# The low parts of the dense weights: subtracted by VectorE alone instead of by VectorE and GpSimd

## The chip, the cores and the metric

The kernel runs on one core of a Trainium2 chip. The metric is the time of one execution on the device in microseconds (us), the median over three runs. Differences are given as a ratio to the kernel before.

## The reference

One block of a streaming encoder, batch 1, 512 tokens of 1024 features, all in float32:

```python
h = rms_norm(x, attn_norm_g);  u = h @ w_in                    # 1024 -> 2048
u_pool, u_q, u_k, u_v = split(u)                               # 512 columns each
y_pool = (trailing means of u_pool over 2/4/8/16 tokens - u_pool) @ w_pool * pool_scale
o = softmax(q1 k1) v - lam * softmax(q2 k2) v                  # 4 heads, two maps each, partial rotary
x += concat(y_pool, rms_norm(o)) @ w_out
x += cross_attention(rms_norm(x), rms_norm(mem), w_cq, w_ckv, w_co)   # 256 rows of memory
x += moe(rms_norm(x))                                          # the top 4 of 32 experts, clamped SwiGLU
return rms_norm(x, final_norm_g)
```

## The kernel before

The program has two stretches. The **dense part** (norms, pooling, differential attention, cross attention, router; about the first 400 us) computes its products in two parts: every operand is split into a high part in float32r (`hi`, rounded by ScalarE) and a low part (`lo`, what is left), and a product is three matmuls, hi*hi, hi*lo and lo*hi (`mm3`). The **experts** follow, one after the other, with plain float32 matmuls; nothing in that stretch is changed.

The dense weights come in 28 pieces of 512 rows by 512 columns (1 MB): 8 of `w_in`, 8 of `w_ckv`, 4 each of `w_out`, `w_cq` and `w_co`. `w_load` (L159) has SyncE issue the DMA of a raw piece into a buffer; `w_split` turns it into `w_hi` and `w_lo`, in two halves `b` = 0 and 1 of 128 partitions x 1024 elements: ScalarE copies to `w_hi` (L117), and an elementwise subtraction of two operands in SBUF gives `w_lo` (L118). `w_next` hands a piece that is ready to the matmuls, splits one ahead and loads one more. The raw piece's buffer is free when both subtractions are done. The normed memory's values, `cv`, are split once in the same way, in two halves `cvs` (L508).

In the kernel before, half 0 is subtracted by VectorE and half 1 by GpSimd, but for the very first piece, which VectorE does alone. So of the 56 subtractions of weights VectorE has 29 and GpSimd 27; both of `cvs` are GpSimd's. Beside these, GpSimd has in the dense part only constants at the start, one small memset (L426) and one small product for the router (L812).

Each engine executes its instructions in the order of the built program, and that order comes from a scheduler: in the dense part it places every instruction by its own estimate of when its inputs and its engine are ready, apart from a short pinned piece at the start. So a change of engine for some instructions also moves others. In the experts the order of TensorE is that of the code.

Names that the rows use: `u` is the pooling branch's product `pps` times the rows' norm (L433), `win` and `mixed` its trailing sums (L572 to L578), `yp` the product with `w_pool`, `y_l` a low part of the block's mixed output (L121). `lams` are the four lambda vectors (L543 to L552). `rot` and `turned` are the rotary step of queries and keys (L280 by ScalarE, L281 to L286 by VectorE), whose result TensorE transposes (`qkT`, L111); `qTl` and `kTl` are low parts of the transposed queries and keys. In the differential attention, `s` are scores, L624 and L625 mask them and take their maximum `mx`, L627 scales it, ScalarE takes the exponential (L629), L631 to L634 make the probabilities `pr`, TensorE transposes them to `aT`, ScalarE copies these to `a` (L643), and L192 to L200 and L658 to L661 (`orstd`, `oss`, `on`) norm the head's output. The products of the memory (`ckps`, `cvps`) are filled in between the steps of this attention.

Of the kernel before, what the change touches and what calls it, by code (L numbers as in the profile page):

```python
# [39 lines left out]
def two_pi_parts():  # L40
    """2*pi cut into parts of at most 12 significant bits."""
    rest, parts = 2 * math.pi, []
    for bits in (9, 20, 31):
        q = math.floor(rest * 2 ** bits) / 2 ** bits
        parts.append(q)
        rest -= q
    parts.append(float(np.float32(rest)))
    return parts


class Halves:
    """A [1024, n] operand, rows k * 128 + p, as float32r high and low parts in four tiles."""
# [8 lines left out]
class Block:  # L61
# [8 lines left out]

    def later(self, n, fn):
        """fn's instructions come n steps of matmuls later."""
        self.todo.append([n, fn])
# [14 lines left out]
    def queued(self):  # L88
        """TensorE's instructions of this block are issued in the order of the program."""
# [9 lines left out]
    @contextmanager  # L99
    def when(self, flag):  # L100
        """TensorE's instructions of this block run if the flag, in a register of its, is set."""
        with self.queued(), self.tc.If(flag):  # L102
            yield
# [9 lines left out]
    def split(self, hi, lo, src, scale=None, lo_engine=None):  # L113
        """src (times a scale per partition) = hi + lo, exactly, both float32r."""
        nc = self.nc
        if scale is None:
            self.pin(nc.scalar.activation(hi, src, AF.Copy))  # L117
            self.pin((lo_engine or nc.vector).tensor_tensor(lo, src, hi.bitcast(F32), op=OP.subtract))  # L118
# [12 lines left out]
    def warm(self, n):  # L131
        """n products that nobody reads: TensorE keeps its clock through a wait."""
        t = self.bank("warm")
        for _ in range(n):
            self.mm(t[:, :P], self.ones, self.ones, start=True, stop=True)
# [13 lines left out]
    # weights of the dense part, in halves [512 rows, 512 columns], in the order of their use  # L149
# [12 lines left out]
    def w_split(self, first=False):  # L162
        if not self.w_raw:
            self.w_load()
        if self.w_raw:
            t = self.w_raw.pop(0)
            hi, lo = self.slot("w_hi", [P, 4, 512], F32R), self.slot("w_lo", [P, 4, 512], F32R)
            for b in range(2):
                c = slice(2 * b, 2 * b + 2)
                self.split(hi[:, c], lo[:, c], t[:, c], lo_engine=self.nc.gpsimd if b and not first else None)  # L170
# [11 lines left out]
    def pin(self, ins):  # L182
        """Where order matters: ins is not issued before what its engine got so far."""
# [3 lines left out]
    def rstd(self, ss, n, name, out=None):  # L187
        """(sum of squares / n + eps) ** -0.5: a first guess from the bits, three Newton steps."""
# [14 lines left out]
    def turn(self, x, g, dst, i, a):  # L203
        """Half a of the features of x [128 rows, 512], times the gain g, to the halves dst, columns
        i * 128 + row."""
# [9 lines left out]
    def squares(self, x, ss):  # L215
        """ss = the sums of the squares of the rows of x."""
# [3 lines left out]
    def gain(self, v, name):  # L220
        """A gain as columns, row k * 128 + p in [p, k]."""
# [16 lines left out]
    def rotary_tables(self, r):  # L238
        """cos, sin [128, 4, 8] of the angles of the positions, and those times r."""
# [32 lines left out]
    def rotary(self, dst, src, i, r=None):  # L272
        """dst [128, 512] = src (PSUM), times r if it is given, with its heads' first 16 columns
        turned."""
# [17 lines left out]
    def tokens_by_piece(self, act, evac, name, before=None, ahead=1):  # L292
        """act.T @ piece for the next two halves of the weights: evac(i, bank) per 128 tokens."""
# [14 lines left out]
    def features_by_piece(self, act, evac, name):  # L308
        """(act.T @ piece).T for the next two halves: evac(f, bank) per 128 features."""
# [11 lines left out]
    def memory_keys(self, act, evac):  # L321
        """The same for the 256 rows of the memory, in steps."""
# [30 lines left out]
    def dense(self):  # L353
# [23 lines left out]
        # the first norm: its gain goes into h, its rows' scales to what comes of h  # L377
# [24 lines left out]
        self.w_split(True)  # L402
# [35 lines left out]
        # queries and keys: turned, then features on partitions  # L438
# [19 lines left out]
        # differential attention, with the memory's keys and values among it  # L458
# [19 lines left out]
        # x += y @ w_out  # L478
# [28 lines left out]
        for n in range(2):  # L507
            self.split(cvs[0][:, n], cvs[1][:, n], cv[:, n], lo_engine=nc.gpsimd)  # L508
# [16 lines left out]
    def columns(self):  # L525
        """pool_scale and subln_g as columns."""
# [11 lines left out]
    def lambdas(self):  # L538
        """The weight of the second map."""
# [14 lines left out]
    def pooling(self, u, cols, y):  # L554
        """Trailing means of u [channel, group, token] less u, times w_pool, to y."""
# [6 lines left out]
        # 1 / (t + 1) for the first tokens  # L562
# [39 lines left out]
    def diff_attention(self, qT, kT, v, y, scale, fill):  # L602
# [3 lines left out]
        def scores(qb, h):  # L606
            n = (qb + 1) * P
            q = slice(qb * P, n)
            # the two maps, [128, n] each, in a bank each
# [73 lines left out]
    def cross_attention(self, cq, ckT, cv, scale):  # L683
# [30 lines left out]
        def turn(i, pr):  # L714
            # pT: tile of two heads, (head, half of the memory)
# [36 lines left out]

    def moe_constants(self):
        nc, c, jp = self.nc, self.cst, self.jp
        # strictly earlier tokens, all tokens
# [10 lines left out]
        # what the one-hot slots pick of a token: its number in two parts, its gate in three, one  # L766
# [14 lines left out]
        # powers of two, for a word of flags per 16 experts  # L781
# [3 lines left out]
        # the gate-up biases, rows (hi or lo, half, expert), and what picks a row of them  # L785
# [33 lines left out]
    def logits(self, i, c):  # L819
        """The sums of squares and the logits of 128 tokens, as far as half c of x goes. The norm  # L820
        is left to route, its gain to what reads the rows and to the router's weights."""
# [19 lines left out]
    def route(self):  # L841
        """The four experts of all tokens, and their places."""
# [37 lines left out]
    def gates(self):  # L880
        """The softmax over the four, in three parts of eight bits."""
# [17 lines left out]
    def count(self):  # L899
        """The experts' numbers of tokens; a word of flags per 16 experts: which have more than  # L900
        64; the number of further passes over an expert with more than 96."""
# [12 lines left out]
        # (pass, expert): a pass over slots 96 pass + 97 and on that has tokens  # L914
# [11 lines left out]
    def load_down_biases(self):  # L926
        """In the room of what the first expert's gate and up get later."""
# [7 lines left out]
    def round_down_biases(self, raw):  # L935
        """The biases of down, a half of the columns each, in rows (high, low, high)."""
# [7 lines left out]
    def down_biases(self, bd):  # L944
        """These and the gates, in rows (high, high, low)."""
# [10 lines left out]
    def one_hots(self, pt, slot_no, tv):  # L956
        """pt [128, 2, 6] = what the slots pick of the tokens"""
# [8 lines left out]
    def slots(self, pt, n):  # L966
        """For the slots of n experts: rows to gather, gates, rows of y to add to."""
# [11 lines left out]
        # a slot without a token matches none  # L979
# [16 lines left out]
    def normed(self, xg):  # L996
        """The rows gathered, times what their norm divides by."""
# [16 lines left out]
    def first_features(self):  # L1014
        """The same for expert 0, straight from x: the others' rows are gathered meanwhile. And the
        gates."""
# [18 lines left out]
    def load_gate_up(self, e, n=KT):  # L1035
        """Rows 8 p + j in tile j, for j < n."""
# [9 lines left out]
    def load_down(self, e):  # L1046
        """Rows 256 j + 2 p + b in tile j."""
# [7 lines left out]
    def swiglu(self, gate, up, n):  # L1055
        """(up + 1) * gate * sigmoid(1.702 gate), clamped; columns (j p b) go to (j b p)."""
# [11 lines left out]
    def biases(self, pick):  # L1068
        """Gate-up accumulators that hold the biases: slots 0..63 on partitions (half of the
        columns, slot), slots 64..95 on (quarter of the columns, slot)."""  # L1070
# [37 lines left out]
    def sums(self):  # L1108
        """Room for what a pair of experts adds: y of slots 0..63 and the tokens' one-hot rows per
        expert, both for slots 64..95 of the two."""  # L1110
# [5 lines left out]
    def down(self, aT, aT2, dn, gat, tok, cond, a, c, last=False):  # L1116
        """gate * act @ w_down and the tokens' one-hot rows: to a for slots 0..63, in partitions
        (high or low part, slot), to c for slots 64..95."""
# [37 lines left out]
    def combine(self, i, parts):  # L1156
        """x += what the parts (rows of y, their tokens' one-hot rows) add to 128 tokens"""
# [243 lines left out]
```

## Time and profile before

| what | value |
|---|---|
| time, median of 3 runs | 1555.97 us (1555.66 to 1556.44) |
| span of the profiled execution, first to last instruction | 1551.3 us |
| TensorE busy | 1491.1 us, 96% of the span |
| VectorE busy | 694.4 us, 45% |
| ScalarE busy | 385.2 us, 25% |
| GpSimd busy | 115.5 us, 7% |
| mean granted clock of TensorE | 0.986 of full speed |

The time of a run is taken around the whole launch, the span from the trace of one execution; they differ by 4.7 us here. A busy share is a mean over very different stretches, so the rows further down are taken by stretch.

### The profile page before, as it was taken

The page shows a single profiled execution, that of the slowest core. Times are in us where ns is not written, and L with a number is a line of the kernel's source. Part 1 is how long each engine was busy: PE and PEld are TensorE (multiplying, and loading weights), DVE is VectorE, ACT ScalarE, POOL GpSimd, SP SyncE. Part 2 cuts the span into 40 slices and gives each one's busy share as a digit, 9 for nine tenths or more (in the row PEclk, how much of TensorE's full clock was granted, in tenths as well). Part 3 has the DMA queues.
Part 4 walks back from the last instruction along what each step waited for, and adds up shares of the span by engine and source line. Part 5 has one row for each costly group of instructions (what it writes and reads, how often), then busy time and mean ns, then how long its engine had stood idle before and what let it go on. Part 6 is the DMA issues. An engine that isn't in the chain of part 4 may idle for free. (4 is left out here: it accounts for less than half of the span.)

```text
span 1551.3 us, 22087 instructions
## 1 busy us (share of the span) xinstructions
PE 1491.1 (96%) x8852; PEld 752.4 (49%) x8852; DVE 694.4 (45%) x1650; ACT 385.2 (25%) x691; POOL 115.5 (7%) x81
## 2 busy tenths in 40 slices
PE   9998999999999999999999999999999999999994
PEld 7777778888733434343433434333343433333332
DVE  6847775352453434243453434343343434444234
ACT  5344544353011111111222111121112111121213
POOL 2212112301000000000000000000000000000001
PEclk9999999999899999999999999999999999999997
DMA  6132124155788998989999998989989999999911
GB/s 218 62 112 82 55 86 150 55 221 203 258 331 319 386 386 341 376 338 399 372 401 404 407 402 326 408 344 360 399 341 390 374 401 373 392 373 389 409 42 56
DMA packets 84152, 455.36 MB, mean 294 GB/s; under 512 B 14169, under 2 KB 14690, under 8 KB 34882
## 3 DMA queue, kind: packets, MB, share of 16 engines
q1 hardware_dynamic: 79170, 438.90, 72.0%
q0 software_dynamic: 3472, 12.29, 2.5%
q10 hardware_dynamic: 1392, 2.51, 0.4%
q8 instruction: 86, 1.41, 0.4%
q14 instruction: 32, 0.26, 0.0%
HBM read 449.45 MB, written 4.21 MB: 292 GB/s over the span
## 5 line engine op out<-in xcount | busy, mean ns | idle before, releaser
L107 PE MATMUL gu<-gu,xT 128*64 128x512 f32 (+1 forms) x3200 | 603.6, 599 | 1.2 <-PEq L102 1.2
L107 PEld LDWEIGHTS gu<-gu,xT 128*64 128x64 f32 (+1 forms) x3200 | 167.9, 127 | 344.9 <-issue 338.4
L107 PE MATMUL down<-dnw,aT 128*32 128x256 f32 (+1 forms) x2288 | 305.0, 478 | 3.3 <-PEq L102 2.5
L107 PEld LDWEIGHTS down<-dnw,aT 128*32 128x32 f32 (+1 forms) x2288 | 108.6, 122 | 175.4 <-issue 149.8
L1105 ACT ACTIVATE aT<-actT 128x512 f32<-128x512 f32 x64 | 27.9, 487 | 542.2 <-PE actT L111 542.2
L1171 DVE TENSOR_TENSOR x<-comb,x 128x1024 f32<-128x1024 f32 x68 | 82.9, 1220 | 131.7 <-PE comb L107 131.7
L1059 DVE TENSOR_SCALAR g<-gu 128x256 f32<-128x256 f32 (+1 forms) x64 | 33.3, 553 | 229.1 <-PE gu L107 193.6
L121 DVE SCALAR_TENSOR_TENSOR yb<-down,gat,yb 32x256 fp32r<-32x256 f32 x128 | 61.6, 481 | 129.5 <-ACT yb L120 129.4
L120 ACT ACTIVATE yb<-down,gat 32x256 fp32r<-32x256 f32 x128 | 59.7, 466 | 224.3 <-PE down L107 118.3
L992 POOL DMA_INDIRECT xg<-x_rows,gi x31 | 28.5, 919 | 1004.9 <-DVE gu L1062 600.0
L107 PE MATMUL comb<-ya,yb 128*128 128x512 f32 x256 | 97.0, 420 | 3.7 <-PEq L102 2.8
L118 POOL TENSOR_TENSOR w_lo<-w,w_hi 128x1024 fp32r<-128x1024 f32 x27 | 71.4, 2647 | 264.1 <-ACT w_hi L117 210.0
L107 PEld LDWEIGHTS comb<-ya,yb 128*128 128x128 f32 x256 | 47.9, 187 | 63.3 <-DVE x L1171 37.8
L121 DVE SCALAR_TENSOR_TENSOR ya<-down,gat,ya 64x512 fp32r<-64x512 f32 x64 | 48.0, 750 | 26.3 <-ACT ya L120 26.2
L117 ACT ACTIVATE w_hi<-w 128x1024 fp32r<-128x1024 f32 x56 | 57.0, 1053 | 10.9 <-DMA w<-in_w_ckv_dram 3.5
L970 DVE COPY slots<-slots 128x12 f32<-128x12 f32 x32 | 5.5, 171 | 118.4 <-PE slots L107 118.4
L1061 ACT ACTIVATE s<-g 128x256 f32<-128x256 f32 (+1 forms) x64 | 32.4, 521 | 87.6 <-DVE g L1059 85.8
L120 ACT ACTIVATE ya<-down,gat 64x512 fp32r<-64x512 f32 x64 | 43.8, 685 | 32.3 <-DVE ya L121 23.8
L107 PE MATMUL comb<-yb,ohc 128*128 128x512 f32 x128 | 50.2, 392 | 0.0
L118 DVE TENSOR_TENSOR w_lo<-w,w_hi 128x1024 fp32r<-128x1024 f32 x29 | 42.1, 1453 | 15.8 <-ACT w_hi L117 13.4
L1065 DVE TENSOR_TENSOR g<-gu,s 128x512 f32<-128x512 f32 (+1 forms) x64 | 48.7, 840 | 0.0
L111 PEld LDWEIGHTS xgT<-ident,xg 96*128 96x128 f32 x248 | 29.9, 202 | 30.6 <-ACT xg L999 16.3
(340 smaller groups left out, 1827.2 us busy)
## 6 DMA issues: line engine op xcount, KB each, us to landing
gu<-in_w_gu_dram SPq DMA_DIRECT2D x256, 1024.0 KB, 12.6
dnw<-in_w_down_dram SPq DMA_DIRECT2D x128, 1024.0 KB, 9.6
w<-in_w_ckv_dram SPq DMA_DIRECT2D x8, 1024.0 KB, 5.1
w<-in_w_in_dram SPq DMA_DIRECT2D x7, 1024.0 KB, 8.1
w<-in_w_out_dram SPq DMA_DIRECT2D x4, 1024.0 KB, 5.0
w<-in_w_cq_dram SPq DMA_DIRECT2D x4, 1024.0 KB, 7.2
w<-in_w_co_dram SPq DMA_DIRECT2D x4, 1024.0 KB, 5.1
x<-in_x_dram SPq DMA_DIRECT2D x8, 256.0 KB, 6.2
```

The lines of the kernel that those rows point to most:

```text
L107: self.pin(self.nc.tensor.matmul(*a, **k))
L111: self.pin(self.nc.tensor.transpose(*a))
L117: self.pin(nc.scalar.activation(hi, src, AF.Copy))
L118: self.pin((lo_engine or nc.vector).tensor_tensor(lo, src, hi.bitcast(F32), op=OP.subtract))
L120: nc.scalar.activation(hi, src, AF.Copy, scale=scale)
L121: nc.vector.scalar_tensor_tensor(lo, src, scale, hi.bitcast(F32), op0=OP.mult, op1=OP.subtract)
L992: nc.gpsimd.indirect_dma_start(out=xg, out_offset=None, in_=self.rows, in_offset=bass.IndirectOffsetOnAxis(ap=gi, axis=0))
L1059: nc.vector.tensor_scalar(g, gate, LIMIT, None, op0=OP.min)
L1061: nc.scalar.activation(s, g, AF.Sigmoid, scale=ALPHA)
L1065: nc.vector.tensor_tensor(g.rearrange("s (j b p) -> s j p b", p=P, b=2), r(up), r(s), op=OP.mult)
L1105: nc.scalar.activation(aT, pt[:, :n], AF.Copy)
L1171: self.nc.vector.tensor_tensor(xi, ps, xi, op=OP.add)
```

## The change

The function that splits loses its choice of engine; VectorE now subtracts both halves of every piece and both halves of the memory's values. (Comments are deleted too, which changes no instruction.)

```diff
-    def split(self, hi, lo, src, scale=None, lo_engine=None):
-        """src (times a scale per partition) = hi + lo, exactly, both float32r."""
+    def split(self, hi, lo, src, scale=None):
+
         nc = self.nc
         if scale is None:
             self.pin(nc.scalar.activation(hi, src, AF.Copy))
-            self.pin((lo_engine or nc.vector).tensor_tensor(lo, src, hi.bitcast(F32), op=OP.subtract))
+            self.pin(nc.vector.tensor_tensor(lo, src, hi.bitcast(F32), op=OP.subtract))
...
-    def w_split(self, first=False):
+    def w_split(self):
...
             for b in range(2):
                 c = slice(2 * b, 2 * b + 2)
-                self.split(hi[:, c], lo[:, c], t[:, c], lo_engine=self.nc.gpsimd if b and not first else None)
+                self.split(hi[:, c], lo[:, c], t[:, c])
...
-        self.w_split(True)
+        self.w_split()
...
         for n in range(2):
-            self.split(cvs[0][:, n], cvs[1][:, n], cv[:, n], lo_engine=nc.gpsimd)
+            self.split(cvs[0][:, n], cvs[1][:, n], cv[:, n])
```

In the built program VectorE has 29 instructions more (27 `w_lo`, 2 `cvsl`) and GpSimd 29 fewer. Three places of VectorE's order show how they come to stand.

The first is VectorE in the pooling branch, from the `u` of the first group on. Before:

```order
L433 TENSOR_TENSOR u<-pps,r_bcast 128x512
L572 TENSOR_TENSOR win<-u 128x511
L573 COPY win<-u 128x1
L118 TENSOR_TENSOR w_lo<-w,w_hi 128x1024
L576 TENSOR_TENSOR mixed<-win,ti 128x1
L578 SCALAR_TENSOR_TENSOR mixed<-win,u 128x511
L433 TENSOR_TENSOR u<-pps,r_bcast 128x512
```

The same place of the changed kernel:

```order
L433 TENSOR_TENSOR u<-pps,r_bcast 128x512
L572 TENSOR_TENSOR win<-u 128x511
L573 COPY win<-u 128x1
L118 TENSOR_TENSOR w_lo<-w,w_hi 128x1024
L433 TENSOR_TENSOR u<-pps,r_bcast 128x512
L576 TENSOR_TENSOR mixed<-win,ti 128x1
L578 SCALAR_TENSOR_TENSOR mixed<-win,u 128x511
L577 TENSOR_TENSOR mixed<-mixed,u 128x1
L572 TENSOR_TENSOR win<-u 128x511
L573 COPY win<-u 128x1
L118 TENSOR_TENSOR w_lo<-w,w_hi 128x1024
L433 TENSOR_TENSOR u<-pps,r_bcast 128x512
```

The second `u` has moved ahead of two rows of `mixed`, and the piece's second `w_lo` stands ahead of the third `u`.

The second place is VectorE where the queries' rotary step begins, after the pooling branch's last `mx`. Before:

```order
L118 TENSOR_TENSOR mx<-mixed,mx 128x512
L546 TENSOR_TENSOR lams<-lams 128x2x64
L121 SCALAR_TENSOR_TENSOR y_l<-yp,cols,y_h 128x512
L269 TENSOR_TENSOR cos_sin<-cos_sin,scales 128x64
L548 TENSOR_REDUCE lame<-lams 128x2
L551 TENSOR_TENSOR lam<-lame 128x1
L552 TENSOR_SCALAR lam<-lam 128x1
L281 TENSOR_TENSOR rot<-qps,cos_sin 128x64
```

In the changed kernel:

```order
L118 TENSOR_TENSOR mx<-mixed,mx 128x512
L269 TENSOR_TENSOR cos_sin<-cos_sin,scales 128x64
L281 TENSOR_TENSOR rot<-qps,cos_sin 128x64
L282 TENSOR_TENSOR rot<-qps,cos_sin 128x64
L283 TENSOR_TENSOR rot<-qps,cos_sin 128x64
L284 TENSOR_TENSOR rot<-qps,cos_sin 128x64
L546 TENSOR_TENSOR lams<-lams 128x2x64
L285 TENSOR_TENSOR turned<-rot 128x8x8
L548 TENSOR_REDUCE lame<-lams 128x2
L286 TENSOR_TENSOR turned<-rot 128x8x8
```

The four rows of `rot` no longer stand behind `lams`, but the first row of `turned` does; the `y_l` that stood here has moved up, and so have two `w_lo` of one piece, where one stood. On SyncE's queue the DMA of the last piece of `w_in` now stands ahead of the DMAs of `lams`, behind which it stood before; it waits there for products of `pps`.

The third place is VectorE at the start of the attention, where the keys' last rotary step meets the first scores. Before, from the last row of `turned` to `kTl` (ahead of these rows the order is that which the changed kernel shows below):

```order
L286 TENSOR_TENSOR turned<-rot 128x8x8
L118 TENSOR_TENSOR w_lo<-w,w_hi 128x1024
L631 RECIPROCAL sums<-sums 128x2
L632 TENSOR_TENSOR sums<-sums,lam 128x1
L118 TENSOR_TENSOR kTl<-qkT,kTh 128x4x128
```

In the changed kernel, from the maximum of the first scores on:

```order
L625 TENSOR_REDUCE mx<-s 128x1 x2
L118 TENSOR_TENSOR w_lo<-w,w_hi 128x1024
L627 TENSOR_SCALAR mx<-mx,scales 128x2
L281 TENSOR_TENSOR rot<-kps,cos_sin 128x64
L282 TENSOR_TENSOR rot<-kps,cos_sin 128x64
L283 TENSOR_TENSOR rot<-kps,cos_sin 128x64
L284 TENSOR_TENSOR rot<-kps,cos_sin 128x64
L285 TENSOR_TENSOR turned<-rot 128x8x8
L286 TENSOR_TENSOR turned<-rot 128x8x8
L118 TENSOR_TENSOR w_lo<-w,w_hi 128x1024
L631 RECIPROCAL sums<-sums 128x2
L118 TENSOR_TENSOR w_lo<-w,w_hi 128x1024
```

Up to `turned` the order is that of before; the added `w_lo` stand behind it, ahead of `kTl`.

## Rows read from the trace of the kernel before

**Rows 1.** The page's first part: busy time, share of the span, instructions.

```profile
PE 1491.1 (96%) x8852; PEld 752.4 (49%) x8852; DVE 694.4 (45%) x1650; ACT 385.2 (25%) x691; POOL 115.5 (7%) x81
```

**Rows 2.** Windows by stretch: busy us per engine, TensorE's granted clock, DMA share, GB/s.

```profile
122.00:210.00 88.00, 74.58 (x466) 62.07 (x466) 69.39 (x184) 44.77 (x104) 19.07 (x7) 0.92 0.24 80
210.00:400.00 190.00, 186.63 (x1064) 159.32 (x1065) 84.73 (x164) 72.44 (x138) 36.22 (x18) 1.00 0.44 160
400.00:1551.00 1151.00, 1117.27 (x6765) 439.61 (x6764) 458.87 (x1068) 210.12 (x366) 35.48 (x34) 0.99 0.88 349
60.00:80.00 20.00, 18.31 (x80) 14.82 (x81) 19.86 (x65) 4.71 (x7) 2.58 (x1) 1.00 0.02 4
```

**Rows 3.** Timeline of TensorE: start, duration, in brackets the idle time before and its releaser.

```profile
61.69 0.50 PE L107 MATMUL pps<-hh,w_hi 128*128 128x512 f32 x1 [2.36 <-DVE u L433]
...
86.06 0.63 PE L111 MATMUL qkT<-ident,turned 128*128 128x128 f32 x4 [2.70 <-DVE turned L286]
...
125.65 0.90 PE L111 MATMUL qkT<-ident,turned 128*128 128x128 f32 x4 [3.66 <-DVE turned L286]
...
141.70 0.39 PE L107 MATMUL s<-kTh,qTh 64*128 64x256 f32 x2 [2.24 <-ACT pr L629]
...
177.19 0.69 PE L107 MATMUL s<-kTh,qTh 64*128 64x384 f32 x1 [3.16 <-ACT a L643]
...
199.91 0.30 PE L111 MATMUL aT<-ident,pr 128*128 128x128 f32 x1 [1.75 <-DVE orstdt L198]
```

**Rows 4.** TensorE's waits, 0 to 400 us: total us, times, longest.

```profile
PE qkT L111 <- DVE turned L286: 6.8, 3, 3.7
...
PE aT L111 <- DVE pr L634: 1.9, 3, 0.9
```

**Rows 5.** Timeline of GpSimd at one of its subtractions.

```profile
56.89 2.40 POOL L118 TENSOR_TENSOR w_lo<-w,w_hi 128x1024 fp32r<-128x1024 f32 x1 [6.17 <-ACT w_hi L117]
```

**Rows 6.** Timeline of VectorE: operations beside those of GpSimd, `u` and `lams`.

```profile
56.94 3.43 DVE L118 TENSOR_TENSOR w_lo<-w,w_hi 128x1024 fp32r<-128x1024 f32 x1
...
60.96 0.68 DVE L433 TENSOR_TENSOR u<-pps,r_bcast 128x512 f32<-128x512 f32 x1
...
74.81 2.37 DVE L573 COPY win<-win 128x8 f32<-128x8 f32 x1
...
83.10 0.29 DVE L546 TENSOR_TENSOR lams<-lams 128x128 f32<-128x128 f32 x1 [1.56 <-DMA lams<-in_lambda_k_dram]
...
119.88 2.62 DVE L118 TENSOR_TENSOR w_lo<-w,w_hi 128x1024 fp32r<-128x1024 f32 x1
...
122.42 2.30 DVE L627 TENSOR_SCALAR mx<-mx,scales 128x2 f32<-128x2 f32 x1
...
138.68 1.88 DVE L627 TENSOR_SCALAR mx<-mx,scales 128x2 f32<-128x2 f32 x1
...
163.58 2.16 DVE L632 TENSOR_TENSOR sums<-sums,lam 128x1 f32<-128x1 f32 x1
...
173.00 2.09 DVE L193 TENSOR_SCALAR orstdt<-orstdv 128x4 int32<-128x4 int32 x1
```

**Rows 7.** VectorE's `w_lo`: duration min/median/max in ns, first and last start.

```profile
L118 DVE TENSOR_TENSOR w_lo<-w,w_hi x29: 1212/1225/3427, 8.4 to 363.6; 128x1024 fp32r<-128x1024 f32 x29
```

**Rows 8.** The page's costliest groups, the weights' subtractions: busy, mean ns | idle before.

```profile
L118 POOL TENSOR_TENSOR w_lo<-w,w_hi 128x1024 fp32r<-128x1024 f32 x27 | 71.4, 2647 | 264.1 <-ACT w_hi L117 210.0
...
L118 DVE TENSOR_TENSOR w_lo<-w,w_hi 128x1024 fp32r<-128x1024 f32 x29 | 42.1, 1453 | 15.8 <-ACT w_hi L117 13.4
```

**Rows 9.** Windows right behind three of TensorE's gaps, columns as above.

```profile
125.80:129.30 3.50, 3.50 (x20) 3.05 (x19) 2.89 (x9) 0.60 (x1) 0.00 (x0) 0.51 0.41 87
142.90:146.30 3.40, 3.40 (x17) 2.98 (x18) 3.37 (x4) 1.41 (x3) 1.70 (x1) 0.50 0.31 119
177.00:183.90 6.90, 6.71 (x18) 5.31 (x19) 4.73 (x20) 2.15 (x6) 0.00 (x0) 0.51 0.00 0
```

**Rows 10.** The page's DMA issues: KB each, median us from issue to landing.

```profile
w<-in_w_in_dram SPq DMA_DIRECT2D x7, 1024.0 KB, 8.1
```

## The prediction

> **What bounds the kernel now.** I read the busy shares first. TensorE works 96% of the span, every other engine less than half, and GpSimd 7% [rows 1]. So a change pays only where TensorE stands still or runs at half clock, and I took the windows by stretch next [rows 2]. In the experts, 400 to 1551 us, TensorE is busy 1117.27 of 1151 us at a granted clock of 0.99; in 210 to 400 it is busy 186.63 of 190. Between 122 and 210 us, the attention, it is busy 74.58 of 88 us at a clock of 0.92, while VectorE works 69.39. In 60 to 80 us VectorE works 19.86 of 20. The experts hold nothing that the change touches, and TensorE bounds them: what the dense part gains or loses moves their start, one to one.
>
> Then the waits of TensorE in the dense part. Its largest gaps stand in its timeline with what ended them [rows 3]: 2.36 us at 61.69 (`u`), 2.70 at 86.06 and 3.66 at 125.65 (`turned`), 2.24 at 141.70 (the exponential `pr`), 3.16 at 177.19 (`a`), 1.75 at 199.91, 15.9 us together. The waits add 0.45 more for `turned` (6.8 less the two) and three for `pr` with 1.9 in sum [rows 4]. All end with VectorE, or with ScalarE behind it. None names a `w_lo`: the subtractions are early enough, and matter only by whom they hold up.
>
> The last view is VectorE beside GpSimd [rows 5, 6]. Half a piece takes VectorE 1.22 us (median) [rows 7]; GpSimd takes 2.65 [rows 8]. But operations of VectorE that start beside one of GpSimd's end only after it. The `w_lo` at 56.94 takes 3.43 us: GpSimd's runs from 56.89 to 59.29, and VectorE ends 1.08 us behind it. The copy of eight columns at 74.81 takes 2.37 us, the scaling of two numbers per partition at 122.42 2.30, and 138.68, 163.58 and 173.00 show 1.88, 2.16 and 2.09 for operations that else take some 0.2. I count 18 such stretched operations in the dense part, by my estimate about 28 us together; seven of them are in these rows (119.88 with 2.62 is the seventh), the others repeat the pattern.
>
> **What the change does, part by part.** It removes 29 subtractions from GpSimd, for which TensorE does not wait, and with them the stretches, some 28 us of VectorE's time. It adds 29 x 1.2 = 35 us to VectorE. That is +7 us on an engine that idles most of the time; what counts is the place of each. ScalarE's copies stay as they are. A piece is done about as early as before (two in sequence, 2.4 us, against one of GpSimd's, 2.65), so raw buffers come free no later, and the loads stay where they are or move up. The two `cvsl` and the 13 `w_lo` behind 210 us lie beside a TensorE that is 98% busy there [rows 2] and waits for none of them; I cost them at nothing. Without that cover they would cost 15 x 1.2 = 18 us.
>
> Place by place, as the order shows them:
> - 61.69, 2.36 us. The stretch of the `w_lo` (3.43 - 1.22 = 2.2 us) goes, and the second `u` stands right behind the first `w_lo`: it ends at 56.94 + 1.22 + 0.68 = 58.8 instead of 60.96 + 0.68 = 61.6 [rows 6]. That is 2.8 earlier, so the gap goes whole: **2.4**.
> - 86.06, 2.70 us. VectorE is full ahead of it. Two stretches go (2.2 each, 56.94 and 74.81), two more `w_lo` stand in the way (2.4), and a `y_l` has moved up (0.7): 1.3 us sooner. Also `rot` no longer stands behind `lams`, whose wait of 1.56 us at 83.10 falls out of its way. That makes up to 3 us, but TensorE itself comes 2.4 sooner. The gap shrinks by 0.5 to 1.8; I take **1.0**.
> - The 0.45 for `turned` behind it comes after another stretched row: **0.45**.
> - 125.65, 3.66 us. Ahead of `turned` stand the `w_lo` at 119.88 with 2.62 us and the scaling at 122.42 with 2.30. Without GpSimd they take 1.2 and 0.2, and the added `w_lo` stand behind `turned`: 1.4 + 2.1 = 3.5, less a little, **3.4**. Behind these `w_lo` waits `kTl`, 1.2 us per `w_lo` later; scores of the last keys need it, and TensorE has products of the memory ahead of them.
> - 141.70, 2.24 us. The scaling at 138.68 loses 1.65 of its 1.88 us, but the second `w_lo` stands ahead of it: 1.65 - 1.2 = **0.45**.
> - The three waits for `pr`, 1.9 us in sum. Each comes after a stretch as that at 163.58 (2.16 - 0.16 = 2.0), and each has one `w_lo` more ahead: up to 0.8 each, or what there is; **1.5**.
> - 177.19, 3.16 us. The stretch of 1.9 at 173.00 goes, and the scaling that lets the exponential start, with `a` behind it in ScalarE's order, now stands ahead of both `w_lo`; some of it is taken by a row of probabilities that has moved ahead: **1.6**.
> - 199.91, 1.75 us: a `w_lo` stretched as the one at 56.94 (2.1) less one of 1.2, and 0.3 by the order of the rows: **1.2**.
>
> That is 12.0 us. Each can be lost again at the next wait: from below I bound the sum by a third, 4 us, since VectorE is full at 60 to 80 us and 79% busy at 122 to 210; from above by all of the gaps named, 18.2 us.
>
> **The clock.** Three gaps are followed by stretches at half clock, 1.2 instead of 2.4 GHz: 0.51 for 3.5 us behind 125.65, 0.50 for 3.4 behind 141.70, 0.51 for 6.9 from 177.0 on [rows 9]. Half of each is lost: 1.7, 1.7 and 3.4 us. The gaps of 2.36 and 2.70 us have no such stretch behind them (60 to 80 us: 1.00 [rows 2]), and one of 2.24 has, so a gap's length alone does not decide. I take back the first (its gap falls to about 0.3 us), 1.7 us, and nothing for the others; from above, all 6.8.
>
> **A rule that speaks against the change.** In 60 to 80 us VectorE is 99% busy [rows 2]. The Trainium skill (Perfetto Trace Analysis, Optimizing Scalar/DVE Operations) says that with VectorE saturated, giving work to GpSimd may make sense, though the port that the two share can undo that. By its first half the two `w_lo` taken back here would cost 2.4 us at 86.06 instead of the 1.0 that I credit, and the sum would be 8.6. The rows show the second half: the two stretches cost VectorE 4.4 us, more than the two `w_lo`.
>
> **The sum.** The profiled execution spans 1551.3 us, with 4.7 us around it by the median. 12.0 + 1.7 = 13.7 us; of these I keep an estimated 12, since many rows change places and some of it is lost again: 1551.3 - 12 = 1539.3 in the span and 1544.0 in time. Less than 0.2% (3.1 us) I call no change, about what a measurement of this kernel can tell.
>
> **The rivals.**
> - No change, within 0.2%. The work added eats the stalls removed, +35 against -28 us on VectorE. Where TensorE waits for a chain of scaling, exponential and `pr`, a `w_lo` of 1.2 in the chain is little better than a stretch; only 61.69 and 125.65 gain (5.8), and half of it is waited for elsewhere: about 1553. For it: the net at 141.70 is only 0.45. Against it: at 125.65 no added `w_lo` stands ahead. Chance 0.13.
> - Part of the gain: 61.69, 86.06 and 125.65 give 6.8, the attention behind gives nothing: 1549, to 1552.9 with a little lost. Chance 0.15.
> - More gain: the half-clock stretches behind 141.70 and 177.19 go as well, 1.7 + 3.4 = 5.1: about 1539, or down to 1533 if all gaps close. For it: these gaps shrink to 1.8 and 1.6. Against it: 2.24 was enough for one. Chance 0.14.
> - Slower. `turned` at 86.06 stands behind `lams`, whose DMAs now queue behind the last 1 MB of `w_in`, and such a piece takes 8.1 us to land [rows 10]. If it starts only when `lams` could, `lams` lands up to 8 us later than at 83.1, `turned` 5 us later than now, and a half-clock stretch follows: the 2.4 of 61.69 and the 1.0 here are lost, 5 + 1.7 to 3.4 come on top, 3.4 at 125.65 come off, and the rest gives nothing: 1559 to 1561. It decides once `lams` lands over 5 us later. For it: VectorE has no slack there. Against it: the piece waits for products of `pps`, which end soon after the gap at 61.69, long before `lams`. Chance 0.08.
>
> **How the numbers follow.** The main case, 1540 to 1549, has 0.50. Under 1536 I put 0.07, over 1556 0.14; the range is 1536 to 1556. Faster by over 0.2%: 0.50 + 0.15 + 0.14 = 0.79; within: 0.13; slower: 0.08.
>
> **What the next profile would show.** If right: no stretched operation on VectorE; `w_lo` x56 there at 1.2 us each; TensorE's gaps at 61 and 125 us gone or under 0.5, that for the first `turned` near 1.7; the stretch 122 to 210 us shorter by some 6 to 8 with a clock over 0.92; the experts' length as before. Wrong if `w_lo` takes VectorE over 1.25 us beside other work, if gaps of over 2 us stand at new places of the attention, or if the experts wait for their weights.

## The result, and the profile after

The changed kernel takes 1530.47 us (median of 4 runs, 1529.61 to 1531.18) against 1555.82 for the kernel before beside it (4 runs, 1554.26 to 1556.44): a ratio of 0.9844, with an interval of 0.9833 to 0.9856. It gained 25.4 us where 12 were predicted; the time lies below the range. The direction was right and so was the mechanism, the size was not. In 40 more runs, beside the experiments, the kernel before takes 1553.5 to 1554.3 us (the medians of four sets); by these the gain is 23 to 24 us.

The page of the kernel after, its first part, answers to [rows 1]; the row of the costliest groups below it to [rows 8]:

```profile
span 1529.3 us, 22025 instructions
...
PE 1482.5 (97%) x8852; PEld 748.6 (49%) x8852; DVE 695.2 (45%) x1679; ACT 385.1 (25%) x691; POOL 39.0 (3%) x52
...
L118 DVE TENSOR_TENSOR w_lo<-w,w_hi 128x1024 fp32r<-128x1024 f32 x56 | 67.0, 1219 | 7.5 <-ACT w_hi L117 7.2
```

GpSimd's 76.5 us are gone, and VectorE, with 29 operations more, is busy 0.8 us longer than before: the work it took over it had lost before in stretched operations. All 56 `w_lo` now take about 1.2 us, also in the busiest stretches. The timeline of VectorE at the third place of the prediction (before: 119.88 with 2.62 us and 122.42 with 2.30, [rows 6]) shows the same operations at 1.22 and 0.22 us:

```profile
115.83 1.22 DVE L118 TENSOR_TENSOR w_lo<-w,w_hi 128x1024 fp32r<-128x1024 f32 x1
116.96 0.22 DVE L627 TENSOR_SCALAR mx<-mx,scales 128x2 f32<-128x2 f32 x1
...
117.75 0.22 DVE L286 TENSOR_TENSOR turned<-rot 128x64 f32<-128x64 f32 x1
117.89 1.22 DVE L118 TENSOR_TENSOR w_lo<-w,w_hi 128x1024 fp32r<-128x1024 f32 x1
```

TensorE's timeline has these gaps left. The first and third stand where 86.06 and 141.70 of [rows 3] stood, and the fourth is a wait of 0.56 us of before (202.90). The second is new: it is the third transpose of `pr`, ahead of which TensorE waited for nothing in before (135.71). Nothing is left of 61.69, 125.65, 177.19 and 199.91:

```profile
82.41 0.63 PE L111 MATMUL qkT<-ident,turned 128*128 128x128 f32 x4 [1.47 <-DVE turned L286]
...
127.92 0.30 PE L111 MATMUL aT<-ident,pr 128*128 128x128 f32 x1 [0.66 <-DVE pr L634]
...
132.41 0.39 PE L107 MATMUL s<-kTh,qTh 64*128 64x256 f32 x2 [0.87 <-ACT pr L629]
...
182.92 0.33 PE L111 MATMUL oT<-ident,on 128*128 128x128 f32 x1 [0.45 <-DVE on L661]
```

Where the time came from is read by windows that begin and end with the first product of the same tile, so that the same work is compared: from the first `pps` to the first `qps`, on to the first `kps`, and from the first `ckps` to the last transposes of `pr` (columns as in [rows 2]). Of before:

```profile
37.01:64.81 27.80, 24.96 (x120) 19.96 (x119) 21.81 (x40) 11.37 (x16) 6.14 (x3) 1.00 0.26 85
64.81:94.52 29.71, 26.56 (x121) 21.32 (x121) 25.64 (x90) 14.20 (x22) 5.09 (x2) 1.00 0.15 46
...
118.95:210.95 92.00, 78.57 (x497) 65.76 (x496) 72.44 (x189) 47.49 (x108) 21.67 (x8) 0.93 0.24 81
```

Of the kernel after, and a window at the start:

```profile
38.70:62.62 23.92, 23.92 (x117) 19.72 (x115) 17.37 (x37) 10.57 (x14) 0.00 (x0) 1.00 0.29 99
62.62:90.42 27.80, 26.33 (x121) 21.47 (x121) 24.46 (x91) 14.38 (x22) 0.00 (x0) 1.00 0.14 44
...
114.89:190.35 75.46, 72.78 (x502) 61.71 (x501) 64.22 (x197) 47.46 (x108) 0.00 (x0) 1.00 0.29 98
...
8.00:12.00 4.00, 2.31 (x8) 2.06 (x9) 3.05 (x3) 1.75 (x3) 0.00 (x0) 0.71 1.00 358
```

The first product of `pps` is 1.7 us later than before: at the start TensorE waits longer for the inputs (1.69 us idle in the last row, at a clock of 0.71). Some 1.0 of this belongs to the one execution: the kernel with more warming products below, which is that of after up to there, has no half clock at the start and its first `pps` at 37.74 us instead of 38.70. Then 3.9 and 1.9 us are won, nothing between `kps` and `ckps`, and 16.5 in the attention; behind it the stretch up to the first `cqps` gives 1.4 more, because five products have moved from there into the attention (502 against 497). The sum is 22.0, the difference of the spans, and past `cqps` it stays. In the attention TensorE's idle time fell from 13.43 us (92.00 - 78.57) to 2.68, that is by 10.75, and its busy time by 5.8, or 7.2 with the products that moved: the granted clock went from 0.93 to 1.00. The rest of the 25.4 is no work: the profiled execution of before stands some 2.7 us under the median of 1555.82 (see the 4.7 us around the span, below), and that of after 0.6 over its own.

### The profile page after: what moved, and what is told of

Read it like the earlier page. It is cut to its first block, busy times and chain, and to the rows that moved or that the text cites. A ratio compares the mean times of both kernels' runs of the same rounds, so it can differ in the third digit from the quotient of the medians.

```text
span 1529.3 us, 22025 instructions
## 1 busy us (share of the span) xinstructions
PE 1482.5 (97%) x8852; PEld 748.6 (49%) x8852; DVE 695.2 (45%) x1679; ACT 385.1 (25%) x691; POOL 39.0 (3%) x52
## 5 line engine op out<-in xcount | busy, mean ns | idle before, releaser
L118 DVE TENSOR_TENSOR w_lo<-w,w_hi 128x1024 fp32r<-128x1024 f32 x56 | 67.0, 1219 | 7.5 <-ACT w_hi L117 7.2
L999 ACT ACTIVATE xg<-xg 96x1024 f32<-96x1024 f32 x31 | 35.6, 1149 | 20.2 <-DMA xg<-x_rows,gi 19.5
```

Of the source, the lines that this page charges most:

```text
L118: self.pin(nc.vector.tensor_tensor(lo, src, hi.bitcast(F32), op=OP.subtract))
L999: self.nc.scalar.activation(xg[:, :D], xg[:, :D], AF.Copy, scale=xg[:, D:D + 1]))
```

## The experiments

The 28 pieces of weights are counted in the order of their splits; GpSimd had the second half of pieces 2 to 28. Pieces 2 to 9 are split ahead of the attention, 10 to 17 in it, 18 to 28 behind. All ratios are to the kernel before, medians to its 1553.5 to 1554.3 us in these runs; "extra" is what a kernel takes over the 1530.5 of after.

**The lock by itself.** By a lock I mean that an operation of one of the two engines lasts until one of the other ends. This kernel is that of after, and GpSimd makes one more subtraction for each piece, whose result nobody reads; VectorE keeps its subtractions.

```diff
                 self.split(hi[:, c], lo[:, c], t[:, c])
+                if b:
+                    self.nc.gpsimd.tensor_tensor(t[:, c], t[:, c], hi[:, c].bitcast(F32), op=OP.subtract)
```

> The changed kernel, with one subtraction more per piece: behind VectorE's second subtraction GpSimd subtracts the high part of half 1 from the raw piece once more, into the raw piece itself, which nobody reads any more. VectorE's order in the dense part is that of the changed kernel but for five rows, so only GpSimd's work beside VectorE comes back, not the order of before. If the stretched operations and what follows them (gaps of TensorE and its half-clock stretches) are the cause, most of the 25 us comes back: 1546 to 1558 us, with VectorE's operations of 0.2 us stretched to about 2 again. If the new order of VectorE's and TensorE's rows is the cause: 1529 to 1533 us.

Measured: 1556.90 us, 1.0023 (1.0014 to 1.0033): the whole gain is gone, with VectorE's order of the changed kernel. The timeline of VectorE and, below, of GpSimd at the place shown above:

```profile
127.17 1.21 DVE L118 TENSOR_TENSOR w_lo<-w,w_hi 128x1024 fp32r<-128x1024 f32 x1
128.29 2.33 DVE L634 TENSOR_TENSOR sums<-sums,lam 128x1 f32<-128x1 f32 x1
...
127.42 3.19 POOL L172 TENSOR_TENSOR w<-w,w_hi 128x1024 f32<-128x1024 f32 x1 [18.65 <-DVE sums L633]
```

A product of one number per partition, else 0.15 us, takes 2.33 and ends with GpSimd's subtraction (130.6 both). GpSimd, which started while a `w_lo` of VectorE ran, takes 3.19 instead of 2.39. TensorE's waits, 0 to 400 us (total, times, longest), show the stall there, where `pr` was 0.9 and `turned` 1.5 in after:

```profile
PE aT L111 <- DVE pr L636: 7.3, 4, 2.4
PE qkT L111 <- DVE turned L288: 5.1, 2, 4.4
```

And its window of the attention, from the first to the last transposes of `pr`:

```profile
131.90:213.90 82.00, 71.99 (x447) 60.17 (x448) 68.29 (x176) 43.24 (x99) 16.89 (x7) 0.92 0.24 78
```

These are 82.00 us at a clock of 0.92. The same window of before has 81.10 at 0.94, that of after 68.10 at 1.00. The stalls hit other operations than in before, so that the loss comes so near to the gain is in part chance; what the run shows is the cause. The window of after:

```profile
121.60:189.70 68.10, 65.87 (x448) 55.52 (x449) 57.53 (x176) 43.20 (x99) 0.00 (x0) 1.00 0.27 94
```

**The same work on VectorE.** One word is another than in the edit above, `vector` for `gpsimd`.

> The changed kernel, with the same third subtraction per piece as in the run with GpSimd's extra one (half 1 of the raw piece once more, into the raw piece, which nobody reads), but on VectorE: 28 x 1.2 = 34 us more of VectorE's own work, and nothing on GpSimd. If a subtraction of 1.2 us in VectorE's order costs about what I charged for each (0.8 to 1.2 us at each of some six places where TensorE waits): 1536 to 1540 us. If such work falls into VectorE's idle time between the steps of a chain, and only a stretch that catches one of the chain's own small operations costs: 1530 to 1533 us. As much as GpSimd's (1557 us) if it is VectorE's time alone that counts.

Measured: 1537.72 us, 0.9895 (0.9878 to 0.9911), 7.2 extra. The total fits the charged case, the place doesn't. The window of the attention:

```profile
127.70:198.40 70.70, 68.72 (x458) 57.51 (x459) 65.64 (x184) 43.72 (x99) 0.00 (x0) 1.00 0.28 90
```

The extra operations in it (count, shortest, median and longest in ns):

```profile
L172 DVE TENSOR_TENSOR w<-w,w_hi x8: 1204/1216/1225, 127.9 to 195.2; 128x1024 f32<-128x1024 f32 x8
```

TensorE's waits, 0 to 400 us:

```profile
PE vps L107 <- ACT hh L117: 3.6, 2, 3.3
...
PE qps L107 <- DVE turned L287: 2.4, 1, 2.4
```

In the attention eight more operations, 9.7 us of VectorE's time, leave TensorE idle for 1.98 us (70.70 - 68.72) where it was 2.23 in after; the window is 2.6 longer because ten more products lie in it. From the first `ckps` to the first `cqps` this kernel takes 124.03 us (121.03 to 245.06) and after 123.60 (114.89 to 238.49). So there a subtraction more costs almost nothing. What is lost is lost ahead of the attention: 6.1 us up to the first `ckps`. There TensorE waits 3.6 us at `vps` and 2.4 at `qps`, 4.9 more than in after (1.1 at `vps`), and half clock follows at both places, which it doesn't in after (windows):

```profile
32.50:39.50 7.00, 6.34 (x16) 4.93 (x17) 4.69 (x9) 3.84 (x6) 0.20 (x1) 0.51 0.00 0
87.00:90.50 3.50, 3.01 (x9) 2.55 (x10) 1.79 (x9) 1.13 (x4) 0.00 (x0) 0.53 0.00 0
```

**Which pieces.** Three kernels give back to GpSimd its half of some pieces only, with this edit and other bounds for `k` (the one from 18 on gives it the two `cvsl` too):

```diff
+            k = self.w_count = getattr(self, "w_count", 0) + 1
...
-                self.split(hi[:, c], lo[:, c], t[:, c])
+                self.split(hi[:, c], lo[:, c], t[:, c], lo_engine=self.nc.gpsimd if b and 2 <= k <= 9 else None)
```

> The changed kernel with GpSimd subtracting half 1 again for pieces 2 to 9 only (split ahead of the attention). If the gain is made place by place where the traces differ, this gives back what lies ahead of the attention, the gaps at 61.69 and 86.06: 3 to 6 us, 1533 to 1537 us. If the stalls ahead pile up into the attention (a later start of every chain), much more: 1540 us and over.

> The changed kernel with GpSimd subtracting half 1 again for pieces 10 to 17 only (split within the attention). If the gain is made in the attention, by its gaps (about 10 us less idle) and its three half-clock stretches (about 7 us), it comes back here: 1544 to 1550 us with a granted clock near 0.92 in that stretch. If the attention's gain came from an earlier start and other order: 1530 to 1536 us.

> The changed kernel with GpSimd subtracting half 1 again for pieces 18 to 28 and both halves of the memory's values. TensorE is 98% busy there in both traces and waits for none of them: no difference to the changed kernel, 1529 to 1532 us. If stretched operations cost time there too, 1533 us or more; if VectorE's added work there costs time, under 1529 us.

Measured: pieces 2 to 9 1536.40 us, 0.9887 (0.9872 to 0.9902), 5.9 extra; pieces 10 to 17 1549.11, 0.9970 (0.9957 to 0.9982), 18.6 extra; from 18 on 1530.31, 0.9845 (0.9831 to 0.9858), nothing. The sum is 24.3 us, where the gain is 23 to 25: the places add up, and what is won at one is not lost at the next. Behind the attention neither assignment costs anything that these runs could tell. TensorE's waits with pieces 10 to 17 on GpSimd:

```profile
PE qkT L111 <- DVE turned L287: 5.1, 2, 3.7
...
PE s L107 <- ACT a L644: 3.1, 1, 3.1
PE s L107 <- ACT pr L630: 2.2, 1, 2.2
PE aT L111 <- DVE pr L635: 1.9, 3, 0.9
PE aT L111 <- DVE orstdt L199: 1.7, 1, 1.7
```

These are the gaps of [rows 3] from 125.65 on, with their lengths of before; the attention, from the first to the last transposes of `pr`, takes 80.00 us at a clock of 0.95. With pieces 2 to 9 on GpSimd the gaps at `u` (2.4) and the first `turned` (2.9) are back, and here a stretch at half clock follows the second (0.66 in 88 to 92 us), which before didn't show.

**Two pieces at a time.** The same edit with 10 to 11, and with 12 to 13.

> The changed kernel with GpSimd subtracting half 1 again for pieces 10 and 11 only, the two beside which the gap of 3.66 us at 125.65 stood. By the terms of the prediction this place gives back 3.4 us of idle time and 1.7 us at half clock: 1534.5 to 1537 us. If the places do not add up (a delay here is waited for later anyway): 1531 to 1533 us. If a delay here goes on into the later steps: over 1538 us.

> The changed kernel with GpSimd subtracting half 1 again for pieces 12 and 13 only, the two beside which the gaps of 2.24 us at 141.70 and 0.45 us at 149.74 stood. By the terms of the prediction, where the second subtraction of VectorE costs nearly what the stretch did, 0.45 + 0.5 us: 1531 to 1532 us. By the two traces (gap of 2.24 against 0.87 us, 0.45 against none, and a half-clock stretch worth 1.7 us): 3 to 4 us, 1533 to 1535 us.

Measured: 1535.23 us, 0.9882 (0.9865 to 0.9898), 4.8 extra, where the terms charge 3.4 + 1.7 = 5.1; and 1533.41, 0.9868 (0.9851 to 0.9884), 2.9 extra, where they charge 0.95. With 10 to 11 the gap at `turned` is 3.69 us, as in [rows 3], and 0.65 of the clock is granted behind it. With 12 to 13 the scores' gap is 1.75 us (TensorE's timeline):

```profile
131.58 0.39 PE L107 MATMUL s<-kTh,qTh 64*128 64x256 f32 x2 [1.75 <-ACT pr L630]
```

Half clock follows (window):

```profile
132.00:136.00 4.00, 4.00 (x21) 3.24 (x20) 3.88 (x11) 3.34 (x8) 1.14 (x1) 0.50 0.60 232
```

Against the 0.87 of after the gap costs 0.9 us, as charged; the other 2 are by this trace the clock (0.54 over 131.5 to 139 us), which the sum had left out here. By difference 18.6 - 4.8 - 2.9 = 10.9 us are left for pieces 14 to 17, which weren't run alone; the terms for the later places give about 4. In the trace with pieces 10 to 17 on GpSimd the gaps of those places are 0.50, 3.15, 1.72 and 0.94, 6.3 us together, and half clock in 172.5 to 176 (0.51) and 316 to 319.5 us (0.52) costs 3.4 more.

**What of GpSimd holds VectorE.** After, with three fills of half a piece by GpSimd for each piece, into a buffer that nobody reads any more: operations that write and read nothing.

```diff
+                if b:
+                    for _ in range(3):
+                        self.nc.gpsimd.memset(t[:, c], 0.0)
```

> The changed kernel, with GpSimd writing zeros three times over half 1 of the raw piece once both subtractions of the piece are done; nobody reads it any more. GpSimd is busy at the same places as with its extra subtraction, but reads nothing from SBUF; VectorE's order is that of the changed kernel but for a few rows. If any work of GpSimd beside VectorE stretches VectorE's operations: near 1557 us, as with the extra subtraction. If only its reads hold up operations of two operands, and its writes only the copies and scalings: 1531 to 1545 us. If writing holds up nothing: 1529 to 1532 us.

Measured: 1536.03 us, 0.9885 (0.9870 to 0.9900), 5.6 extra. The timeline beside one set of fills:

```profile
117.75 2.98 POOL L173 MEMSET w<- 128x1024 f32 x3 [17.18 <-DVE sums L634]
118.66 0.15 DVE L635 TENSOR_TENSOR sums<-sums,lam 128x1 f32<-128x1 f32 x1
118.73 0.68 DVE L118 TENSOR_TENSOR kTl<-qkT,kTh 128x512 fp32r<-128x512 f32 x1
119.33 0.47 DVE L636 TENSOR_SCALAR pr<-pr,sums 128x128 f32<-128x128 f32 x1
...
120.44 1.22 DVE L118 TENSOR_TENSOR w_lo<-w,w_hi 128x1024 fp32r<-128x1024 f32 x1
```

Operations of two tensors keep their 0.15, 0.68 and 1.22 us beside the fills: of 40 that start beside one in the dense part, none takes over 0.01 us more than usual. The scaling of `pr` takes 0.47 instead of 0.28, and others up to 0.8 us more. So it is GpSimd's reading that holds operations of two inputs, while scalings are held by its fills too, each of which takes 0.95 us and not 2.4. The Trainium skill says the same (SBUF — State Buffer, Who interferes with whom): one pair of ports is shared, whoever issues first keeps it for the whole instruction, two-input operations meet GpSimd's reads only, and scalings may want the whole pair. The trace agrees in what it can show, the 2.33, 3.19 and 0.47 us above; the ports themselves no run here shows. The fills also keep the raw buffer about as long as the extra subtraction did, so a buffer that comes free later isn't what cost 26 us.

**Shorter locks.** Before's assignment, but GpSimd subtracts half a piece in four operations of 128x256 (`cvsl` on VectorE):

```diff
+                for n in range(4):
+                    r = slice(128 * n, 128 * n + 128)
+                    lo_engine.tensor_tensor(lo[:, :, r], src[:, :, r], hi[:, :, r].bitcast(F32), op=OP.subtract)
```

> GpSimd subtracts half 1 of every piece but the first, as before the change, but in four instructions of 128 x 256 elements instead of one of 1024; the memory's values stay with VectorE. If VectorE waits only until the instruction of GpSimd that is under way ends, a stretch falls from some 2.1 to at most 0.7 us, and most of the gain stays: 1532 to 1541 us. If it waits until GpSimd has no more work queued, or the total of GpSimd's work counts: 1550 to 1557 us.

Measured: 1543.47 us, 0.9929 (0.9915 to 0.9942), 13.0 extra, which neither case expected. No operation is stretched by more than 0.6 us, but many are; VectorE beside two such sets, which run from 116.69 to 124.2:

```profile
117.55 1.65 DVE L123 TENSOR_TENSOR w_lo<-w,w_hi 128x1024 fp32r<-128x1024 f32 x1
119.12 0.70 DVE L633 TENSOR_SCALAR mx<-mx,scales 128x2 f32<-128x2 f32 x1
...
121.16 1.76 DVE L123 TENSOR_TENSOR w_lo<-w,w_hi 128x1024 fp32r<-128x1024 f32 x1
```

By addition over 0 to 400 us, each operation's time over the median of its form in all these kernels where it is over 0.1 us, VectorE loses 28.7 us in before (18 operations), 26.0 in the kernel with GpSimd's extra subtractions (17), 14.7 with pieces 10 to 17 there (9), 19.8 here (43), 9.9 beside the fills (21) and none in after. The extra times are some 23 to 25, 26.4, 18.6, 13.0 and 5.6 us. So neither the number of stalls nor their sum gives the price: 19.8 us in short stalls cost less here than 14.7 in long ones at the attention, and from piece 18 on 3.6 us cost nothing. The place counts as well.

**The clock by itself.** The kernel before, with 24 products that nobody reads ahead of the two scores whose gaps half clock follows:

```diff
         def scores(qb, h):
+            if (qb, h) in ((1, 0), (2, 3)):
+                self.warm(24)
```

> The kernel before, with 24 small products that nobody reads put ahead of two groups of scores, those at which TensorE waits for 2.24 us (141.70) and 3.16 us (177.19), so that it works through these gaps; GpSimd and VectorE are as before the change. The gaps' own length stays. If the half-clock stretches behind these two gaps cost their 1.7 and 3.4 us because TensorE stood still: 3 to 6 us less than before, 1548 to 1551 us, with a granted clock of 1.00 behind them. If the clock falls for another reason: no difference or some 2 us more, from the added products.

Measured: 1558.02 us, 1.0031 (1.0019 to 1.0043), slower by 3.7. It failed as a test:

```profile
174.95 1.50 PE L107 MATMUL warm<-ones 128*128 128x128 bf16 x24
179.63 0.44 PE L107 MATMUL s<-kTh,qTh 64*128 64x384 f32 x2 [3.18 <-ACT a L645]
```

The products ran at once and the gap stood behind them as long as before, so half clock followed as before. It says nothing on what the clock is worth.

**The gap that is left.** After, with the operations and DMAs of `lams` issued before the rotary tables:

```diff
+        self.lambdas()
         self.rotary_tables(rs[:, 0])
...
-        self.lambdas()
         self.tokens_by_piece(h, turned(qT), "qps")
```

> The changed kernel with the four lambda vectors loaded and reduced ahead of the rotary tables, so that the first turned queries no longer stand behind them. If the gap of 1.47 us at 82.41 that is left in the changed kernel is the wait for these vectors: it falls to about 0.5 us and the time to 1528 to 1530 us. If it is set by the full VectorE or by ScalarE's tables there: no difference, 1529.5 to 1532 us.

Measured: 1532.19 us, 0.9854 (0.9839 to 0.9870): no gain. The gap of 1.47 went, and 1.5 at `u` and 0.5 at `turned` came. By the timelines of ScalarE and VectorE it isn't `lams` that `turned` waits for in after, but the table of cosines, which comes behind a load of ScalarE's function tables; no run here tests that:

```profile
78.80 1.28 ACT L268 ACT_TABLE_LOAD   x1
...
80.85 0.23 DVE L269 TENSOR_TENSOR cos_sin<-cos_sin,scales 128x64 f32<-128x64 f32 x1 [1.34 <-ACT cos_sin L267]
```

**The half clock ahead of the experts.** After, with 86 warming products instead of 64 ahead of `place`, where a wait of 1.2 us stands:

```diff
-        self.warm(64)
+        self.warm(86)
```

> The changed kernel with 86 instead of 64 small products ahead of the placing of the tokens, so that TensorE stands still there for nearly nothing instead of 1.25 us; nothing of the weights is changed. Both kernels show TensorE at half clock for about 13.7 us behind this gap, which costs 6.8 us. If the gap brings that on: 1522 to 1527 us. If it comes from the many small products around it, or from the step to the experts: no difference, 1529 to 1532 us.

Measured: 1531.00 us, 0.9852 (0.9836 to 0.9869), the same time. The wait is closed, and half clock comes all the same, from 381 us on, with TensorE busy throughout (the 64 products `xgT`):

```profile
378.00:382.00 4.00, 4.00 (x18) 4.00 (x18) 0.71 (x3) 0.31 (x1) 0.00 (x0) 0.94 1.06 311
382.00:386.00 4.00, 4.00 (x18) 4.00 (x18) 2.38 (x7) 0.63 (x1) 0.00 (x0) 0.50 1.00 363
```

That stretch is in all the kernels here, and its cause stays open.

## Why the prediction was right in direction and too small

The steps that failed are two terms of the sum, both too small: the clock, with 1.7 us where the stretches at half clock that went are worth 6.8, and TensorE's waits in the attention behind 125.65, with 4.75 where 7.1 went. The 4.7 us around the span and the 1.7 taken off the sum did the rest. The steps one by one; the sums of the trace are those of the windows above.

- **The mechanism** held. GpSimd's subtractions hold VectorE, VectorE's chain holds TensorE; the same extra work costs 26.4 us on GpSimd and 7.2 on VectorE.
- **61.69, 2.4:** right, the gap is gone; the stretch up to `qps` gave 3.9, since a wait of 0.5 for `r_diag` went too and TensorE's products, three fewer of them by the records, took 1.0 less.
- **86.06, 1.0, and the 0.45:** the gap went from 2.70 to 1.47 (1.2), and the stretch gave 1.9. But what is left of it is no `w_lo` and not `lams`, so that the size came out is in part luck.
- **125.65, 3.4, with 1.7 of clock:** right, 5.1 charged against 4.8 measured.
- **141.70, the three `pr`, 177.19 and 199.91, 4.75 together:** too small. Measured, 2.24 fell to 0.87 (1.4 where 0.45 was charged), and the three `pr`, 177.19 and 199.91 went whole, with a new wait of 0.66 and some under 0.3; at 177.19 that is 3.2 where 1.6 was charged. At 141.70, the `pr` and 199.91 the prediction charged the second `w_lo` with up to 1.2 us, as if it stood in the chain. By the traces it stands mostly in time in which VectorE would wait anyway, though no run tests this `w_lo` by itself. ScalarE's waits for the scaled maxima, in the window of the attention, were in before

```profile
ACT pr L629 <- DVE mx L627: 28.0, 11, 5.1
```

and in after

```profile
ACT pr L629 <- DVE mx L627: 9.7, 9, 1.9
```

  18.3 us shorter with 16 `w_lo` on VectorE there instead of eight; with eight operations more again TensorE waited no longer. So the attention's idle time fell by 10.75, 3.66 of it at 125.65, where 8.15 (3.4 with these 4.75) were charged.
- **The clock, 1.7:** the larger mistake. All three stretches of [rows 9] went, worth 6.8 by their lengths; with the products that moved, TensorE's busy time fell by 7.2. The rival "more gain" said so at 0.14 and with too little, because I held the remaining gaps at 1.8 and 1.6 us; they are 0.87 and nothing. These lengths are those of one execution each; as a price of the clock by itself the 6.8 are not shown. That the 2.70 us had no half clock behind them is right, but not by the window of [rows 2] that is named for it: 64.81 to 94.52 us, above, shows it.
- **13.7 kept as 12:** unfounded, as the pieces add up (24.3 us of 23 to 25).
- **4.7 us around the span:** wrong by 2.9. Every run of before and after beside the experiments and the result shows 1.7 to 1.85 us, those of the other kernels up to 2.1 (1531.06 of time at a span of 1529.3; runs of before 1553.25 at 1551.5). I had set the median of other executions against one profiled execution, which by that was one of about 1553.1.
- **Nothing behind 210 us, and the experts one to one:** right; GpSimd may have all of those pieces at no cost, and the lead of 22 us stays the same from `cqps` on.
- **The rival "slower":** it did not come; `lams` had landed when VectorE came to it (at 81.52 us in after, without a wait), so the loads moved past each other without harm.

From 1544.0 to 1530.5 are 13.5 us: 2.9 around the span, 1.7 of the discount, 6.7 in the attention (16.5 - 8.15 - 1.7), 1.95 ahead of it, 1.4 behind it and 0.6 by which the profiled run of after stands over its median, less 1.7 lost at the start.

The rule that was weighed (the Trainium skill, Perfetto Trace Analysis, Optimizing Scalar/DVE Operations) says that with VectorE full it may make sense to give GpSimd work, and that with the port that the two share it might not help. Its first half would have made the gain smaller; the runs agree with its warning: in the window where VectorE was 99% busy [rows 2], 60 to 80 us, TensorE stood still for 1.69 us in before, and with the work taken back from GpSimd it runs through. The window of after:

```profile
60.00:80.00 20.00, 20.00 (x89) 16.21 (x88) 18.86 (x67) 6.26 (x8) 0.00 (x0) 1.00 0.18 59
```

## What to carry to other kernels

An operation on GpSimd that reads two tensors beside VectorE is paid by VectorE's chain: look in VectorE's timeline for tiny operations of 2 us that end with GpSimd's, and ask of each whether TensorE waits behind it (of 28.7 us in before, those in the attention cost most, those behind it nothing). An operation added to VectorE cost less than its length here, where VectorE waits for other engines within each step of a chain, so look at its idle time between the steps before charging it. And when several gaps of a stretch shrink together, put the clock behind all of them into the range, not only that behind the one that closes by the sum.

## What was not expected of the hardware

- The lock holds GpSimd too: 3.19 us for a subtraction that takes 2.39, when VectorE's began first.
- Fills by GpSimd, which read nothing, hold VectorE's scalings (0.47 us instead of 0.28, and once 1.01 instead of 0.22), but not its operations of two tensors.
- TensorE's clock doesn't follow from the gap's length. The 2.36 us at `u` are followed by no half clock in before and with pieces 2 to 9 on GpSimd, and by one in the kernel of before with warming products, which come only later. The waits of 1.05 and 0.8 us around 300 us, at `pT` and `co`, are followed by none in after (1.00 in 300.7 to 304.2 us), and by one in the kernel with more warming products, which is that of after up to there (the second row). Behind 1.75 us it came elsewhere. So a stretch of 3.5 us at half clock more or less in a trace, 1.7 us, need not come from the change. Ahead of the experts the clock fell with no gap at all.

```profile
61.50:65.00 3.50, 3.30 (x8) 2.63 (x9) 3.50 (x11) 0.63 (x1) 0.00 (x0) 0.52 0.00 0
...
299.50:303.00 3.50, 3.40 (x16) 3.40 (x17) 3.06 (x8) 2.73 (x9) 0.00 (x0) 0.51 1.01 428
```
